# Attention logits from high and low halves: three products instead of four, the last as two 64-row matmuls

## The chip, the core and the metric

The kernel runs as one program on one core of one Trainium2 chip. The metric is the device time of one execution in microseconds (us). Five engines work side by side, each through its own queue in order: TensorE (PE in the profile, with its weight loads listed apart as PEld), VectorE (DVE), ScalarE (ACT), GpSimd (POOL) and SyncE (SP), which here only starts transfers (DMA).

## The reference, cut to what matters

One encoder layer is applied to two sequences, a prompt of 1024 rows and a sample of 2048 rows, both of width 1024. After a projection to eight parts, two attentions run over different parts:

```python
# window_gqa: 8 heads of 64, 2 key heads, blocks of 128 queries against 3 blocks of 128 keys
logits = einsum('bnqhgd,bnkhd->bnhgqk', qb, kw) * (HEAD_DIM ** -0.5)
logits = where(valid, logits + bias, NEG_INF);  p = softmax with a sink
# diff_attention: 4 heads, each with two maps (m) of 64, every query against all S keys
logits = einsum('bqhmd,bkhmd->bhmqk', qb, kh) * (HEAD_DIM ** -0.5)
p = softmax(logits + bias);  w = p[:, :, 0] - lam * p[:, :, 1]
out = rms_norm(einsum('bhqk,bkhe->bqhe', w, vh)) * (1 - lambda_init)
```

Then come a gate, the output projection and a layer norm. The contraction of every logit runs over only 64 elements.

## The kernel before, in words

All large matmuls run in a rounded 32-bit form (F32R). To keep accuracy, each operand is split in a high part and a low part, x = xH + xL, each rounded by itself, and a product is summed from several matmuls of the parts.

**Stages.** First the modulation and the input projections (`projections`, `step3`, lines 187 to 189: three matmuls of 128 rows by 512 columns for each step). Queries and keys go to DRAM in both parts: a tile's first 64 rows are high, the next 64 are low. In the last third of the projections the windowed attention (`windowed`, `first`, `second`) is interleaved with them: `beside()` sends projection steps to PE between its pieces. Then comes the differential attention (`slot`, `logits`, `transpose`, `values`), the sample's 4 heads first (64 units of 128 queries), then the prompt's (16 units, each of two blocks of queries against 1024 keys). Its first three units (EARLY) run among the last projections. The output projection (`outputs`) ends the kernel.

**Windowed logits.** For each head `first` takes one PSUM tile `lgA` of two and adds two matmuls of 128 rows: the weights are the head's queries [qH; qL], the moving side is the keys' high part in both halves of the partitions, then the low part in both halves (line 608). A VectorE pass (line 610) adds the bias and takes the minimum, and ScalarE takes the exponential.

**Differential logits.** A slot j of four in a unit works on one map m and half the keys: a PSUM tile `lg` of 128 by 1024 (two banks, c = 0 and 1), and for each bank two matmuls of 128 rows by 512 columns (line 822): the queries [qH; qL] (v = 0) and the same with the halves swapped, [qL; qH] (v = 1), both against [kH; kL]. That gives high by high, low by low, and both mixed products. VectorE adds the bias (line 827), ScalarE takes the exponential (835), GpSimd combines the two maps (844, 846). Three units later PE transposes the result (860), ScalarE and VectorE split it (862, 863), and PE multiplies it with the values (878 to 880).

**What sets the order.** PE's order around the change is written out by hand (`manual_schedule(engines={PE})`): in a slot the logits, then up to six value matmuls, then four transposes. The other engines' orders come from the framework's planner, which simulates the program. All transfers are started on SP's queue. Queries of the differential attention arrive in two layouts already (lines 780 to 782: the second one swapped by two transfers of 64 partitions each). Keys come by `load_keys` (line 751), the windowed queries by `load_block` (line 588).

Of the kernel before, what the change touches and what calls it, by code (L numbers as in the profile page):

```python
# [11 lines left out]
F32 = mybir.dt.float32  # L12
# [8 lines left out]
P = 128  # L21
D = 1024
KC = D // P
HD = 64
# [13 lines left out]
CH = 512  # L38
# [29 lines left out]
def hybrid_layer(ctx, tc, x_prompt, x_sample, c_prompt, c_sample, w_in, w_out, w_ada, b_ada, ln_g, ln_b,  # L68
                 attn_sink, lambda_q1, lambda_k1, lambda_q2, lambda_k2, subln_w, rel_bias, oh, eye,
                 y_prompt, y_sample):  # L70
    nc = tc.nc
# [3 lines left out]
    def pool(stack, name, bufs=1, space=None, side=None):  # L75
        if space is None:
            return stack.enter_context(tc.tile_pool(name=name, bufs=bufs, side=side, reuse_waits="tile"))
        if space == DRAM:
            return stack.enter_context(tc.tile_pool(name=name, bufs=bufs, space=space))
        return stack.enter_context(tc.tile_pool(name=name, bufs=bufs, space=space, side=side, reuse_waits="tile"))  # L80
# [15 lines left out]
    QA, KA, VA, GA, QB, KB, VB, GB, OT, OA = ([] for _ in range(10))  # L96
# [291 lines left out]
    def fill(n):  # L388
        for _ in range(n):
            next(steps, None)  # L390
# [110 lines left out]
    with tc.issue_after(wload[6]):  # L501
# [15 lines left out]
        for i in range(2):  # L517
            bg = sm2.tile([1, D], F32, tag="bg", name="bg")
            nc.sync.dma_start(out=bg, in_=b_ada[2 * D:3 * D].rearrange("(o d) -> o d", o=1))
            for q in range(2):  # L520
                cs = slice(q * 512, (q + 1) * 512)
# [12 lines left out]
    def windowed(upto):  # L534
# [3 lines left out]
        Bs, live, wait, n0 = {}, [], [], done.get(2, 0)  # L538
        total = (upto - n0) * 32
        Bs[0] = load_block(*order[0])  # L540
        count = [0, 0]

# [29 lines left out]
    def load_keys_of(s, i):  # L572
        T = SEQS[s] // P
        lo, hi = max(i - 1, 0), min(i + 1, T - 1)
        nb = hi - lo + 1
        nk = nb * P
        K = kv_p.tile([P, 2, 2, 384], F32R, tag="k", name="KAt")
        src = KA[s][:, :, :, lo * P:lo * P + nk].rearrange("n l d t -> d n l t")
        nc.sync.dma_start(out=K[0:HD, :, :, :nk].bitcast(F32), in_=src)
        nc.sync.dma_start(out=K[HD:P, :, :, :nk].bitcast(F32), in_=src)  # L580
        V = kv_p.tile([P, 3, 2 * P], F32R, tag="v", name="VAt")
        return dict(s=s, i=i, nb=nb, nk=nk, lo=lo, boff=(lo - (i - 1)) * P, K=K, V=V, l={})

    def load_block(s, i):
        B = load_keys_of(s, i)
        cs = slice(i * P, (i + 1) * P)
        B["Q"] = qa_p.tile([P, HA, P], F32R, tag="q", name="QAt")
        nc.sync.dma_start(out=B["Q"].bitcast(F32), in_=QA[s][:, :, cs].rearrange("h r t -> r h t"))
        k0, nb = B["lo"] * P, B["nb"]
        nc.sync.dma_start(out=B["V"][:, :nb].bitcast(F32),  # L590
                          in_=VA[s][k0:k0 + nb * P, :].rearrange("(b p) e -> p b e", p=P))
        B["G"] = qa_p.tile([P, 4, P], F32, tag="g", name="GAt")
        nc.sync.dma_start(out=B["G"], in_=GA[s][:, :, cs].rearrange("i r t -> r i t"))
        return B

    def first(B, n):

        nk, boff = B["nk"], B["boff"]
        nm = sA_p.tile([P, 4], F32, tag="nm", name="nmA")
        sm_ = sA_p.tile([P, 4], F32, tag="sm", name="smA")  # L600
        l = l_p.tile([P, 4, 386], F32, tag="l", name="l")
        nc.scalar.copy(l[:, :, 0:1], nsink[:, n * 4:n * 4 + 4].unsqueeze(2))
        B["l"][n] = l
        for h4 in range(4):
            h = n * 4 + h4
            L = ps_lgA.tile([P, 512], F32, tag="lgA", name="lgA")
            for hl in range(2):
                nc.tensor.matmul(L[:, :nk], lhsT=B["Q"][:, h, :], rhs=B["K"][:, n, hl, :nk],  # L608
                                 start=(hl == 0), stop=(hl == 1))
            nc.vector.tensor_tensor_reduce(  # L610
                out=l[:, h4, 1:1 + nk], in0=L[:, :nk], in1=tA[:, h, boff:boff + nk], scale=1.0,
                scalar=nsink[:, h:h + 1], op0=ALU.add, op1=ALU.min, accum_out=nm[:, h4:h4 + 1])
            nc.scalar.activation(l[:, h4, :1 + nk], l[:, h4, :1 + nk], AF.Exp, bias=nm[:, h4:h4 + 1], scale=-1.0,
                                 accum_out=sm_[:, h4:h4 + 1])
            if h4 == 3:
                rc = sA_p.tile([P, 4], F32, tag="rc", name="rcA")
                nc.vector.reciprocal(out=rc, in_=sm_)  # L617
                for q in range(4):
                    lv, r1 = l[:, q, 1:1 + nk], rc[:, q:q + 1]
                    if q == 1:  # L620
                        nc.scalar.activation(lv, lv, AF.Copy, scale=r1)
                    else:
                        nc.gpsimd.tensor_scalar(out=lv, in0=lv, scalar1=r1, scalar2=1.0, op0=ALU.mult, op1=ALU.mult)  # L623
            yield

    def second(B, n):
# [5 lines left out]
        def values(b):  # L632
            H, L = parts[b]
            v = B["V"][:, b, n * P:(n + 1) * P]
            nc.tensor.matmul(O, lhsT=v, rhs=H, start=(b == 0), stop=False)
            nc.tensor.matmul(O, lhsT=v, rhs=L, start=False, stop=(b == nb - 1))  # L636

        for b in range(nb + 2):
            if b > 1:
                values(b - 2)  # L640
            if b < nb:
# [3 lines left out]
                H = pa_p.tile([P, 512], F32R, tag="pth", name="pthA")  # L645
                L = pa_p.tile([P, 512], F32R, tag="ptl", name="ptlA")
                nc.scalar.copy(H, pt)
                nc.vector.tensor_tensor(out=L, in0=pt, in1=H.bitcast(F32), op=ALU.subtract)
                parts.append((H, L))
# [22 lines left out]
    ps_lgA = pool(ast, "ps_lgA", 2, PSUM)  # L672
# [54 lines left out]
    for s in (1, 0):  # L727
        T = SEQS[s] // P
        for h in range(HB):
            for i in range(0, T, 2):  # L730
                g = len(groups_of)
                n = len(units)
# [15 lines left out]
    def load_keys(s, h, some):  # L748
        for kq in some:
            kt = k_p.tile([P, 2, CH], F32R, name="kt")  # L750
            nc.sync.dma_start(out=kt.bitcast(F32),
                              in_=KB[s][h][:, :, kq * CH:(kq + 1) * CH].rearrange("m r t -> r m t"))
            heads[s, h][1].append(kt)

    def load_head(s, h):
# [41 lines left out]
    def logits(n, j):  # L797

        s, h, i, g = units[n]
        if n == j == 0:  # L800
            load_head(s, h)
            load_keys(s, h, range(2, SEQS[s] // CH))
            load_queries(g)
            fill(25)
        m, hf = 1 - j // 2, j % 2
        G = groups_[g]
        W, Kt, _ = heads[s, h]
        if "s0" not in G:
            G["s0"] = st_p.tile([P, 2], F32, tag="s0", name="s0g")
        if j == 0:  # L810
            rows[n] = {}
            stats[n] = (st_p.tile([P, 2, 2], F32, tag="nm", name="nm"), st_p.tile([P, 8], F32, tag="s1", name="s1"))
        if hf == 0:
            rows[n][m] = (r1_p if m else r0_p).tile([P, SMAX], F32, name=f"l{m}")
        nm, s1 = stats[n]
        row = rows[n][m]

        b, kt0 = (i % 2, hf * 2) if s else (hf, 0)
        L = ps_lg.tile([P, 1024], F32, name="lg")
        for c in range(2):  # L820
            for v in range(2):
                nc.tensor.matmul(L[:, c * CH:(c + 1) * CH], lhsT=G["Q"][:, v, m, b * P:(b + 1) * P],  # L822
                                 rhs=Kt[kt0 + c][:, m, :], start=(v == 0), stop=(v == 1))
        off = (1 - i) * P + hf * 1024 + LC if s else (1 - i - hf) * P + LC
        off = min(max(off, 0), LC + 384)
        half = row[:, hf * 1024:(hf + 1) * 1024]
        nc.vector.tensor_tensor_reduce(  # L827
            out=half, in0=L, in1=W[:, off:off + 1024], scale=1.0,
            scalar=nm[:, m, 0:1] if s and hf else 3e38, op0=ALU.add, op1=ALU.min, accum_out=nm[:, m, hf:hf + 1])
        if s and hf == 0:  # L830
            return
        c = 0 if s else hf
        sums = s1[:, c:c + 1] if m else G["s0"][:, b:b + 1]
        e = row if s else half
        nc.scalar.activation(e, e, AF.Exp, bias=nm[:, m, hf:hf + 1], scale=-1.0, accum_out=sums)  # L835
        if m == 1:
            nc.vector.reciprocal(out=s1[:, 2 + c:3 + c], in_=sums)
            return
        r = s1[:, 4 + c:5 + c]
        nc.vector.tensor_scalar(out=r, in0=sums, scalar1=s1[:, 2 + c:3 + c], scalar2=neglam, op0=ALU.mult,  # L840
                                op1=ALU.mult)
        for c in range(2) if s else (hf,):
            cs = slice(c * 1024, (c + 1) * 1024)
            nc.gpsimd.tensor_scalar(out=rows[n][1][:, cs], in0=rows[n][1][:, cs], scalar1=r, scalar2=1.0,  # L844
                                    op0=ALU.mult, op1=ALU.mult)
            nc.gpsimd.tensor_tensor(out=row[:, cs], in0=row[:, cs], in1=rows[n][1][:, cs], op=ALU.add)  # L846
# [322 lines left out]
```

## Time and profile before

| What | Value |
|---|---|
| median of 3 runs | 2135.27 us (2133.46 to 2138.25) |
| the profiled execution's own time | 2139.87 us |
| its span in the trace | 2138.1 us |
| PE busy | 2069.9 us, 97% |
| PEld busy | 1779.8 us, 83% |
| DVE busy | 1297.1 us, 61% |
| POOL busy | 1162.2 us, 54% |
| ACT busy | 1040.4 us, 49% |
| mean granted TensorE clock | 0.987 of full speed |

Busy time is the union of an engine's instructions. Matmuls are pipelined: the record of one lasts longer than the distance to the next, so PE's pace is read from the starts, and a busy PE is not one at its peak. The shares are means over the whole span; the stages differ, so the stretches are looked at one by one below.

### The profile page before, as it was taken

What the parts mean: (1) busy time and instruction counts of PE and PEld (TensorE: products, weight loads), DVE (VectorE), ACT (ScalarE), POOL (GpSimd) and SP (SyncE); (2) the same over time, 40 slices, a digit from 0 to 9 for tenths busy, and PEclk for the clock granted to TensorE, in tenths of its full rate; (3) what the DMA queues carried; (4) which work ended last, traced back from release to release, by engine and by line L of the source; (5) the groups of instructions that cost most, each with busy time, mean ns of one, the idle gap of its engine ahead of it and who ended that gap; (6) DMA issues with size and microseconds to landing.
All of it is one profiled execution on the core that took longest, in us unless ns stands there. A gap on an engine that the chain in (4) does not pass through costs nothing.

```text
span 2138.1 us, 32629 instructions
## 1 busy us (share of the span) xinstructions
PE 2069.9 (97%) x11597; PEld 1779.8 (83%) x11597; DVE 1297.1 (61%) x2534; ACT 1040.4 (49%) x2022; POOL 1162.2 (54%) x840
## 2 busy tenths in 40 slices
PE   7999999999999999999997999999999999699998
PEld 4777898888988888888886999999999998688887
DVE  5325224212225777677653999999999998455555
ACT  5211103011015777677632777777777897422221
POOL 3213213212124344343342889898898889777774
PEclk9999999999999999999998999999999999799999
DMA  9675635435538868778435123132231486767763
GB/s 270 180 258 182 181 128 167 130 124 135 154 117 226 203 173 213 196 209 216 144 113 161 38 81 78 47 101 57 84 77 38 116 163 84 140 163 204 196 195 103
DMA packets 340203, 312.46 MB, mean 146 GB/s; under 512 B 32086, under 2 KB 296950, under 8 KB 339656
## 3 DMA queue, kind: packets, MB, share of 16 engines
q1 hardware_dynamic: 340040, 310.37, 53.7%
q8 instruction: 92, 1.51, 0.4%
q14 instruction: 71, 0.58, 0.2%
HBM read 212.70 MB, written 97.60 MB: 145 GB/s over the span
## 4 chain that ended last, share of the span: by engine, by line
PE 85%; DMA 7%; POOL 2%; DVE 2%; issue 2%; ACT 1%; SPq 1%; DVEq 0%; POOLq 0%; ACTq 0%
PE lg L822 13%; PE pj L187 12%; PE pj L188 12%; PE pj L189 12%; PE tp L860 6%; PE po L1048 4%; PE po L1050 4%; PE po L1049 4%; PE ac L880 3%; PE ac L879 3%; PE ac L878 3%; PE lgA L608 3%; PE tp L644 3%; DMA Q<-qb 2%; PE ac L636 2%
## 5 line engine op out<-in xcount | busy, mean ns | idle before, releaser
L187 PE MATMUL pj<-uH,wH 128*128 128x512 f32 x1040 | 418.7, 403 | 6.0 <-DVE gg L258 6.0
L218 POOL TENSOR_TENSOR wL<-wr,wH 128x1024 fp32r<-128x1024 f32 x74 | 181.8, 2459 | 418.1 <-DVE wH L216 377.0
L189 PE MATMUL pj<-uH,wL 128*128 128x512 f32 x1040 | 407.7, 392 | 0.0
L188 PE MATMUL pj<-uL,wH 128*128 128x512 f32 x1040 | 407.1, 391 | 0.0
L822 PE MATMUL lg<-kt,Q 128*128 128x512 f32 x1280 | 379.3, 418 | 16.7 <-DMA Q<-qb 15.0
L846 POOL TENSOR_TENSOR l<-l,l 128x1024 f32<-128x1024 f32 x160 | 383.1, 2415 | 1.2
L835 ACT ACTIVATE l<-l,nm 128x2048 f32<-128x2048 f32 (+1 forms) x192 | 331.0, 1724 | 16.7 <-DVE nm L827 16.1
L822 PEld LDWEIGHTS lg<-kt,Q 128*128 128x128 f32 x1280 | 219.2, 191 | 48.3 <-issue 15.0
L844 POOL TENSOR_SCALAR l<-l,s 128x1024 f32<-128x1024 f32 x160 | 178.3, 1127 | 126.2 <-DVE s L840 68.3
L827 DVE CUSTOM_DVE_ANT_0 l<-lg,W 128x1024 f32<-128x1024 f32 x192 | 233.3, 1215 | 18.8 <-PE lg L822 18.4
L862 ACT CAST pth<-tp 128x512 fp32r<-128x512 f32 x320 | 186.2, 582 | 113.6 <-PE tp L860 108.5
L189 PEld LDWEIGHTS pj<-uH,wL 128*128 128x128 f32 x1040 | 195.5, 188 | 42.3
L187 PEld LDWEIGHTS pj<-uH,wH 128*128 128x128 f32 x1040 | 196.0, 188 | 39.2 <-DVE gg L258 6.8
L863 DVE TENSOR_TENSOR ptl<-tp,pth 128x512 fp32r<-128x512 f32 x320 | 209.2, 685 | 25.7 <-ACT pth L862 23.6
L188 PEld LDWEIGHTS pj<-uL,wH 128*128 128x128 f32 x1040 | 196.3, 189 | 31.0
L860 PE MATMUL tp<-ident,l 128*128 128x128 f32 x1280 | 195.0, 276 | 14.1 <-DVE ptl L863 14.1
L623 POOL TENSOR_SCALAR l<-l,rcA 128x384 f32<-128x384 f32 (+1 forms) x144 | 81.0, 581 | 190.7 <-DVE rcA L617 97.3
L880 PE MATMUL ac<-pth,vt 128*128 128x256 f32 x640 | 182.3, 285 | 0.0
L879 PE MATMUL ac<-ptl,vt 128*128 128x256 f32 x640 | 181.5, 284 | 0.0
L878 PE MATMUL ac<-pth,vt 128*128 128x256 f32 x640 | 181.2, 283 | 0.0
L827 DVE CUSTOM_DVE_ANT_0 l<-lg,W,nm 128x1024 f32<-128x1024 f32 x128 | 164.1, 1282 | 24.1 <-PE lg L822 17.0
L860 PEld LDWEIGHTS tp<-ident,l 128*128 128x128 f32 x1280 | 150.2, 142 | 17.0 <-DVE ptl L863 10.7
(210 smaller groups left out, 4031.6 us busy)
## 6 DMA issues: line engine op xcount, KB each, us to landing
wr<-in_w_in SPq DMA_DIRECT2D x39, 1024.0 KB
KAt<-ka SPq DMA_DIRECT2D x40, 384.0 KB
QAt<-qa SPq DMA_DIRECT2D x24, 512.0 KB
kt<-kb SPq DMA_DIRECT2D x24, 512.0 KB
Q<-qb SPq DMA_DIRECT2D x48, 256.0 KB
Q<-qb SPq DMA_DIRECT2D x96, 128.0 KB
vt<-vb SPq DMA_DIRECT2D x48, 256.0 KB
wa<-in_w_ada SPq DMA_DIRECT2D x32, 256.0 KB
```

Source lines behind the costliest of these rows:

```text
L187: nc.tensor.matmul(acc, lhsT=a(k), rhs=b(k), start=(k == 0), stop=False)
L188: nc.tensor.matmul(acc, lhsT=a(k), rhs=bl(k), start=False, stop=False)
L189: nc.tensor.matmul(acc, lhsT=al(k), rhs=b(k), start=False, stop=(k == KC - 1))
L822: nc.tensor.matmul(L[:, c * CH:(c + 1) * CH], lhsT=G["Q"][:, v, m, b * P:(b + 1) * P], rhs=Kt[kt0 + c][:, m, :], start=(v == 0), stop=(v = ...
L827: nc.vector.tensor_tensor_reduce(out=half, in0=L, in1=W[:, off:off + 1024], scale=1.0, scalar=nm[:, m, 0:1] if s and hf else 3e38, op0=ALU ...
L835: nc.scalar.activation(e, e, AF.Exp, bias=nm[:, m, hf:hf + 1], scale=-1.0, accum_out=sums)
L846: nc.gpsimd.tensor_tensor(out=row[:, cs], in0=row[:, cs], in1=rows[n][1][:, cs], op=ALU.add)
L860: nc.tensor.transpose(pt[:, c * P:(c + 1) * P], rows[n][0][:, (j * 4 + c) * P:(j * 4 + c + 1) * P], ident)
L863: nc.vector.tensor_tensor(out=L[:, :, qs], in0=p3, in1=H[:, :, qs].bitcast(F32), op=ALU.subtract)
L878: nc.tensor.matmul(a, lhsT=Vt[kq][:, 0, c, :], rhs=H[:, c, :], start=(kb == 0), stop=False)
L879: nc.tensor.matmul(a, lhsT=Vt[kq][:, 0, c, :], rhs=L[:, c, :], start=False, stop=False)
L880: nc.tensor.matmul(a, lhsT=Vt[kq][:, 1, c, :], rhs=H[:, c, :], start=False, stop=(kb == T - 1))
```

## The change: what it does

In both attentions the product of the two low parts is dropped. What is left for a logits tile is the two mixed products, or one mixed and the high one, in one matmul of 128 rows, and one product over 64 rows.

In the differential attention, bank c = 0 takes the swapped queries [qL; qH] against [kH; kL], which gives both mixed products; bank c = 1 takes the plain queries [qH; qL] against keys that are now stored swapped, [kL; kH]. After these two come two matmuls of 64 rows, high by high: bank 0 on partitions 0 to 63, bank 1 on partitions 64 to 127. For this `load_keys` loads every odd chunk of 512 keys with its halves swapped, by two transfers of 64 partitions in place of one.

In the windowed attention two heads are taken together, in both `lgA` tiles at once: two matmuls of 128 rows ([qH; qL] against the keys' high part in both halves), then two of 64 rows (qH against the keys' low part), the even head's on partitions 0 to 63 and the odd head's on 64 to 127. Odd heads' queries are loaded swapped, so `load_block` starts three transfers where it started one. VectorE's and all later work is the same.

```diff
@@ load_block
-        nc.sync.dma_start(out=B["Q"].bitcast(F32), in_=QA[s][:, :, cs].rearrange("h r t -> r h t"))
+        qe, qo = [QA[s].rearrange("(h e) r t -> e r h t", e=2)[e][:, :, cs] for e in range(2)]
+        q4 = B["Q"].rearrange("r (h e) t -> r h e t", e=2).bitcast(F32)
+        nc.sync.dma_start(out=q4[:, :, 0], in_=qe)
+        nc.sync.dma_start(out=q4[0:HD, :, 1], in_=qo[HD:P])
+        nc.sync.dma_start(out=q4[HD:P, :, 1], in_=qo[0:HD])
@@ first
-            L = ps_lgA.tile([P, 512], F32, tag="lgA", name="lgA")
-            for hl in range(2):
-                nc.tensor.matmul(L[:, :nk], lhsT=B["Q"][:, h, :], rhs=B["K"][:, n, hl, :nk],
-                                 start=(hl == 0), stop=(hl == 1))
+            if h4 % 2 == 0:
+                Ls = [ps_lgA.tile([P, 512], F32, tag="lgA", name="lgA") for _ in range(2)]
+                for e in range(2):
+                    nc.tensor.matmul(Ls[e][:, :nk], lhsT=B["Q"][:, h + e, :], rhs=B["K"][:, n, 0, :nk],
+                                     start=True, stop=False)
+                for e in range(2):
+                    rs = slice(e * HD, (e + 1) * HD)
+                    nc.tensor.matmul(Ls[e][:, :nk], lhsT=B["Q"][rs, h + e, :], rhs=B["K"][rs, n, 1, :nk],
+                                     start=False, stop=True)
+            L = Ls[h4 % 2]
@@ load_keys
-            nc.sync.dma_start(out=kt.bitcast(F32),
-                              in_=KB[s][h][:, :, kq * CH:(kq + 1) * CH].rearrange("m r t -> r m t"))
+            src = KB[s][h][:, :, kq * CH:(kq + 1) * CH].rearrange("m r t -> r m t")
+            if kq % 2:
+                nc.sync.dma_start(out=kt[0:HD].bitcast(F32), in_=src[HD:P])
+                nc.sync.dma_start(out=kt[HD:P].bitcast(F32), in_=src[0:HD])
+            else:
+                nc.sync.dma_start(out=kt.bitcast(F32), in_=src)
@@ logits
+        qs = slice(b * P, (b + 1) * P)
         for c in range(2):
-            for v in range(2):
-                nc.tensor.matmul(L[:, c * CH:(c + 1) * CH], lhsT=G["Q"][:, v, m, b * P:(b + 1) * P],
-                                 rhs=Kt[kt0 + c][:, m, :], start=(v == 0), stop=(v == 1))
+            nc.tensor.matmul(L[:, c * CH:(c + 1) * CH], lhsT=G["Q"][:, 1 - c, m, qs], rhs=Kt[kt0 + c][:, m, :],
+                             start=True, stop=False)
+        for c in range(2):
+            rs = slice(c * HD, (c + 1) * HD)
+            nc.tensor.matmul(L[:, c * CH:(c + 1) * CH], lhsT=G["Q"][rs, c, m, qs], rhs=Kt[kt0 + c][rs, m, :],
+                             start=False, stop=True)
```

## Rows read from the trace of the kernel before

**Rows 1.** The page's chain that ended last: shares of the span by engine and line.

```profile
PE 85%; DMA 7%; POOL 2%; DVE 2%; issue 2%; ACT 1%; SPq 1%; DVEq 0%; POOLq 0%; ACTq 0%
```

**Rows 2.** Busy time by stretch: windowed attention, then three stretches of the differential one.

```profile
core 0: us, PE busy (x) PEld busy (x) DVE busy (x) ACT busy (x) POOL busy (x), PEclk, DMA share, GB/s
670.00:1050.00 380.00, 376.39 (x2035) 319.39 (x2033) 268.58 (x709) 270.25 (x688) 151.26 (x181) 1.00 0.77 198
...
1250.00:1650.00 400.00, 400.00 (x2701) 366.00 (x2700) 370.42 (x711) 313.82 (x523) 352.16 (x220) 1.00 0.27 74
1650.00:1750.00 100.00, 100.00 (x681) 91.66 (x679) 94.03 (x199) 88.19 (x181) 90.12 (x59) 1.00 0.56 128
1750.00:1820.00 70.00, 65.03 (x434) 59.25 (x433) 58.06 (x132) 57.06 (x127) 60.62 (x41) 0.98 0.63 97
```

**Rows 3.** Groups by line with shapes kept apart: busy us, mean ns.

```profile
L822 PE MATMUL lg<-kt,Q 128*128 128x512 f32 x1280 | 379.3, 418 | 16.7 <-DMA Q<-qb 15.0 <-DVE gg L258 1.4 <-DVE nm L827 0.3
...
L608 PE MATMUL lgA<-KAt,QAt 128*128 128x384 f32 x320 | 84.6, 345 | 0.0
...
L608 PE MATMUL lgA<-KAt,QAt 128*128 128x256 f32 x64 | 13.1, 286 | 0.0
```

**Rows 4.** PE over one slot of the differential attention: start us, length us.

```profile
1502.04 0.60 PE L860 MATMUL tp<-ident,l 128*128 128x128 f32 x4
1502.40 1.16 PE L822 MATMUL lg<-kt,Q 128*128 128x512 f32 x4
1503.40 0.28 PE L878 MATMUL ac<-pth,vt 128*128 128x256 f32 x1
1503.51 0.28 PE L879 MATMUL ac<-ptl,vt 128*128 128x256 f32 x1
...
1504.11 0.60 PE L860 MATMUL tp<-ident,l 128*128 128x128 f32 x4
1504.47 1.18 PE L822 MATMUL lg<-kt,Q 128*128 128x512 f32 x4
```

**Rows 5.** PE where windowed logits stand between projections.

```profile
902.54 0.51 PE L608 MATMUL lgA<-KAt,QAt 128*128 128x384 f32 x2
902.88 0.39 PE L187 MATMUL pj<-uH,wH 128*128 128x512 f32 x1
```

**Rows 6.** PE, line 473's own lengths (ns min/median/max), and weight loads around it.

```profile
97.47 0.39 PE L188 MATMUL pj<-uL,wH 128*128 128x512 f32 x1
97.70 0.39 PE L189 MATMUL pj<-uH,wL 128*128 128x512 f32 x1
98.02 1.02 PE L473 MATMUL ac<-ohs,rbx 33*8 33x512 f32 x2
98.97 0.50 PE L187 MATMUL pj<-uH,wH 128*128 128x512 f32 x1
99.31 0.39 PE L188 MATMUL pj<-uL,wH 128*128 128x512 f32 x1
...
L473 PE MATMUL ac<-ohs,rbx x4: 588/590/592, 98.0 to 107.8; 33*8 33x512 f32 x2, 33*4 33x512 f32 x2
...
97.48 0.19 PEld L189 LDWEIGHTS pj<-uH,wL 128*128 128x128 f32 x1
98.02 0.09 PEld L473 LDWEIGHTS ac<-ohs,rbx 33*8 33x8 f32 x2 [0.35 <-issue]
98.97 0.19 PEld L187 LDWEIGHTS pj<-uH,wH 128*128 128x128 f32 x1 [0.86 <-DVE eL L285]
99.08 0.19 PEld L188 LDWEIGHTS pj<-uL,wH 128*128 128x128 f32 x1
```

**Rows 7.** PE around the 4-row matmuls of line 452.

```profile
48.91 0.40 PE L189 MATMUL ac<-uH,wL 128*128 128x512 f32 x1
49.24 1.05 PE L452 MATMUL pmt<-sel,mrow 4*128 4x2 f32 x8
50.22 0.50 PE L187 MATMUL ac<-uH,wH 128*128 128x512 f32 x1
50.55 0.40 PE L188 MATMUL ac<-uL,wH 128*128 128x512 f32 x1
```

**Rows 8.** PE around the 128-row, 2-column matmuls of lines 525 and 526.

```profile
185.92 0.39 PE L189 MATMUL pj<-uH,wL 128*128 128x512 f32 x1
186.15 0.40 PE L525 MATMUL ac<-gH,onesr 128*2 128x512 f32 x1
186.38 0.40 PE L526 MATMUL ac<-gL,onesr 128*2 128x512 f32 x1
186.62 0.39 PE L187 MATMUL pj<-uH,wH 128*128 128x512 f32 x1
```

**Rows 9.** Waits of PE from 1650 to 1830: us in total, times, longest.

```profile
PE tp L860 <- DVE ptl L863: 3.8, 4, 1.4
PE lg L822 <- DMA Q<-qb: 3.5, 1, 3.5
```

**Rows 10.** DMA issues on SP's queue by line: lines 588, 780 and 781, ns min/median/max.

```profile
L588 SPq DMA_DIRECT2D QAt<-qa x24: 359/366/1351, 219.7 to 1022.0; - x24
L780 SPq DMA_DIRECT2D Q<-qb x48: 359/360/2000, 1061.8 to 1789.2; - x48
L781 SPq DMA_DIRECT2D Q<-qb x48: 579/579/1707, 1063.4 to 1790.1; - x48
```

## The prediction

> **What bounds the kernel now.** I read first the chain that ended last: 85% of the span is PE's, every other engine at most 2%, DMA 7% [rows 1]. Then the busy time by stretch, because the change touches two stages only. In the windowed stage PE is busy 376.4 of 380 us and no other engine passes 75%; in the sample's part of the differential attention PE is busy 400 of 400 us, but VectorE stands at 370.4 (93%) and GpSimd at 352.2 (88%) close behind [rows 2]. So PE's time is the kernel's time in both places, and in the second there is little room before VectorE is the bound. [...] Last I read PE's own starts, since its records overlap: four logits matmuls take from 1502.40 to the next value matmul at 1503.40, and a slot's period is 2.07 us [rows 4]. A matmul of 128 rows by 512 columns in a run of equals takes 0.23 us from start to start (97.47 to 97.70), and its weights are loaded during the one before it (97.48) [rows 6].
>
> **What goes.** 1280 logits matmuls in the differential attention make 320 tiles of four [rows 3]. If the two 64-row matmuls of a tile share one pass, one pass of 0.23 us goes from each: 320 x 0.23 = 73.6 us. In the windowed attention 384 matmuls make 96 pairs of heads, 80 with 384 columns and 16 with 256. A pass of 384 columns takes (902.88 - 902.54) / 2 = 0.17 us [rows 5]; one of 256 takes 0.12 (1503.40 to 1503.51, [rows 4]). That is 80 x 0.17 + 16 x 0.12 = 15.5 us. So 89 us of PE's passes go at most.
>
> **What comes: the crossings.** The new order on PE goes from 128 rows to 64 and back once in each tile and pair. The trace before has no 64-row F32R matmul, but it has PE crossing from 128 rows to fewer and back, at line 473 (33 rows) and line 452 (4 rows). In: the matmul after 97.70 does not start 0.23 later but at 98.02, 0.32 later, and its weight load starts only then, not at 97.70 [rows 6]; at 48.91 to 49.24 it is 0.33 [rows 7]. So 0.09 us are lost and the load is no longer hidden. Out: line 473's second record starts at 98.02 + 1.02 - 0.59 (the median length of one record) = 98.45 and, with 0.43 between the two, its pass ends at 98.88; the next load and matmul start at 98.97, 0.09 later. That matmul's record is 0.50 instead of 0.39 and the next one starts 0.34 after it instead of 0.23: the uncovered load costs 0.11 [rows 6]. The same 0.50 and 0.33 follow line 452 [rows 7]. A round trip of F32R matmuls of 128 columns of weights therefore costs 0.09 + 0.11 + 0.09 + 0.11 = 0.40 us. Changing only the columns, 128 to 2 and back, costs nothing: the starts stay 0.23 apart [rows 8].
>
> Two doubts. Lines 452 and 473 are also the kernel's only products in full 32 bits, so the wait could belong to that form and not to the rows; the transposes, full 32 bits too, meet F32R matmuls without such a gap (0.36 for four, [rows 4]), so I take it for the rows. If it is not, a crossing costs 0. And the second half's weights have to be loaded too, 0.11 if after the first half's, 0 if beside it; no row shows two loads into different rows, so I take the middle, 0.05.
>
> [...]
>
> **The sum.** A differential tile: 0.40 + 0.05 - 0.23 = +0.22 us; 320 x 0.22 = 70.4. PE was idle some 5 us in the prompt's part (7.3 us of waits, [rows 9]), and this takes up added time: 65. A windowed pair: 0.40 + 0.05 - 0.17 = +0.28 (80 of them) or 0.40 + 0.05 - 0.12 = +0.33 (16): 27.7. Together +93 us on the profiled execution's 2139.9, so 2233; the median lies 4.6 us under that execution, which gives 2228.
>
> **Edits at nothing.** The transfers: `load_block` starts three instead of one, 24 times, at 0.36 to 0.58 us of SP's queue each [rows 10], some 0.8 to 1.2 us more in a block that lasts about 16 us (380 / 24), a block ahead of its use; 12 odd key chunks are two transfers instead of one. Bytes and row lengths stay. Prefetch hides them; uncovered they would cost at most 24 x 1.2 = 29 us, and less than nothing isn't to be had. What queues behind them on SP are the block's values and gates, needed later still. The wait for two free `lgA` tiles instead of one: PE has projections between its logits in this stage [rows 5], and VectorE is at 71% [rows 2], so both tiles are long free; if not, PE's queue waits for one more pass of line 610, with projections held behind it. VectorE, ScalarE and GpSimd do the same work in the same shapes. That the planner lays their orders out anew I put at 0, give or take 5 us.
>
> **The rivals.** *No crossing cost, VectorE becomes the bound (faster).* The 64-row loads are pulled ahead and the halves run together. PE's unit of four slots falls from 8.28 to 8.28 - 4 x 0.23 = 7.36 us. VectorE needs 0.926 x 8.28 = 7.67 for a unit [rows 2], so it decides from there. It works in order and waits for ScalarE inside the unit, so I put it at 97% busy: 7.91. The sample's 61 units after the early three gain 61 x 0.37 = 23 us, the prompt's part (VectorE at 94%) 5, the early three units 12 x 0.23 = 3, the windowed pairs 15.5: 47 us, 2088. With VectorE at 100% it is 2071, with no gain in the differential attention 2116. For it: that the wait at lines 452 and 473 may be the 32-bit form's. Against it: every crossing of rows that I looked at has the wait, in both directions.
>
> [...]
>
> *The halves run one after the other (slower still).* Then no pass is saved, the second load hides behind the first half, and each round trip costs its 0.40: 320 x 0.40 - 5 + 96 x 0.40 = 161, so 2296. This is also the case in which the change doesn't do what it says. For it: no row shows two matmuls in the array at once. [...]
>
> *The wait without the uncovered loads.* Only 2 x 0.09 are paid: 0.18 - 0.23 = -0.05 for a tile, about 0 for a pair: 320 x -0.05 = -16, so 2119; with half of the loads uncovered 0.18 + 0.11 + 0.05 - 0.23 = +0.11, 35 us, and about 15 more from the pairs: 2185.
>
> **How the numbers follow.** The forecast, crossings as in rows 6 and 7 with the halves side by side, 0.45: 2228, its own range 2205 (second load hidden: 0.17 a tile, 0.23 or 0.28 a pair, +72) to 2253 (second load in full: 0.28, 0.34 and 0.39, +118). VectorE as the bound 0.37: 2071 to 2116. The wait without loads or with half of them 0.10: 2115 to 2190. One after the other 0.08: around 2296. Range 2075 to 2258: it leaves out the last case, a little of the fastest and the odd case above, under 0.2. Measurement can tell about 0.2% (4 us) from no change. Faster: 0.37 and half of 0.10, 0.42; slower: 0.45, 0.08 and nearly half of 0.10, 0.55; the same 0.03.
>
> **What would show it.** In the changed trace: in a slot, the first 64-row matmul about 0.32 us after the second mixed one, with its load at the same moment; the two 64-row starts about 0.1 apart; the next value matmul about 0.9 to 0.95 us after the second mixed one (0.69 before); a record of 0.39 in place of 0.28 for that value matmul; a slot's period of about 2.29 us with PE busy throughout and VectorE down to some 84%. The forecast is wrong if the loads of the 64-row matmuls start with the matmul before them, if the period falls under 2.07 with VectorE near 97%, or if the 64-row starts lie 0.23 or more apart.

## The result and the profile after

The changed kernel takes 2207.18 us (median of 4 executions; one of them, 4091.93 us, was disturbed and is left out of the ratio) against 2136.76 us before: 1.0314 times as long, 95% interval 1.0295 to 1.0333. That is +70 us; +93 was forecast, in a range that holds the measured time. The profiled execution took 2199.95 us, 2198.2 of it in the span.

One slot of the changed kernel on PE, and a narrower window that shows the second mixed matmul's own start (start us, length us):

```profile
1501.08 0.60 PE L880 MATMUL tp<-ident,l 128*128 128x128 f32 x4
1501.44 0.71 PE L838 MATMUL lg<-kt,Q 128*128 128x512 f32 x2
1502.08 0.50 PE L842 MATMUL lg<-kt,Q 64*128 64x512 f32 x2
1502.52 0.39 PE L898 MATMUL ac<-pth,vt 128*128 128x256 f32 x1
1502.74 0.28 PE L899 MATMUL ac<-ptl,vt 128*128 128x256 f32 x1
...
1503.34 0.60 PE L880 MATMUL tp<-ident,l 128*128 128x128 f32 x4
1503.69 0.72 PE L838 MATMUL lg<-kt,Q 128*128 128x512 f32 x2
...
1501.76 0.40 PE L838 MATMUL lg<-kt,Q 128*128 128x512 f32 x1
```

The weight loads of the same slot, and the 64-row matmuls' own lengths over the whole kernel (ns min/median/max):

```profile
1501.41 0.30 PEld L838 LDWEIGHTS lg<-kt,Q 128*128 128x128 f32 x2
1502.08 0.19 PEld L842 LDWEIGHTS lg<-kt,Q 64*128 64x128 f32 x2 [0.37 <-issue]
1502.51 0.19 PEld L898 LDWEIGHTS ac<-pth,vt 128*128 128x128 f32 x1 [0.25 <-issue]
...
L842 PE MATMUL lg<-kt,Q x640: 490/496/793, 1096.6 to 1878.2; 64*128 64x512 f32 x160
```

To be seen here, beside [rows 4]: the period is 2.25 us (1501.44 to 1503.69) where it was 2.07, though a pass is gone. The second mixed matmul starts at 1501.76 and the 64-row pair at 1502.08, 0.32 later instead of 0.23, with its loads only then. The pair's two records together last 0.50, and one alone 0.496: they start together (3 to 4 ns apart by the trace's own starts, in all 416 pairs), and so do their loads (two in 0.19, one is 0.18). The value matmul behind them starts at 1502.52 with a record of 0.39 instead of 0.28, and its load again starts with it, not before.

The same stretches as in [rows 2], the later ones moved to where the stage now lies:

```profile
670.00:1050.00 380.00, 378.10 (x1922) 288.12 (x1920) 257.04 (x673) 255.19 (x655) 144.61 (x174) 1.00 0.75 194
...
1300.00:1700.00 400.00, 398.03 (x2494) 291.07 (x2493) 351.92 (x657) 289.75 (x483) 322.58 (x202) 1.00 0.25 65
1700.00:1800.00 100.00, 100.00 (x630) 73.20 (x628) 88.26 (x182) 81.27 (x157) 86.77 (x56) 1.00 0.52 114
```

PE is as full as before and gets less done: 2494 instead of 2701 matmuls in 400 us. VectorE (third pair) falls from 370 to 352 us and GpSimd from 352 to 323, so neither set the pace. The granted clock is 1.00 in all three stretches.

### The profile page after: what moved, and what is told of

Read it like the earlier page. It is cut to its first block, busy times and chain, and to the rows that moved or that the text cites. A ratio compares the mean times of both kernels' runs of the same rounds, so it can differ in the third digit from the quotient of the medians.

```text
span 2198.2 us, 32677 instructions
## 1 busy us (share of the span) xinstructions
PE 2134.6 (97%) x11597; PEld 1672.3 (76%) x11597; DVE 1311.1 (60%) x2534; ACT 1037.5 (47%) x2022; POOL 1160.2 (53%) x840
## 4 chain that ended last, share of the span: by engine, by line
PE 87%; DMA 6%; DVE 2%; POOL 2%; issue 1%; SPq 1%; ACT 1%; DVEq 0%; POOLq 0%; ACTq 0%
PE pj L187 12%; PE pj L188 11%; PE pj L189 11%; PE lg L838 7%; PE lg L842 6%; PE tp L880 6%; PE ac L898 6%; PE po L1068 4%; PE po L1070 4%; PE po L1069 4%; PE ac L900 3%; PE ac L899 3%; PE tp L655 3%; PE ac L646 2%; PE lgA L618 2%; PE ac L647 1%
## 5 line engine op out<-in xcount | busy, mean ns | idle before, releaser
L187 PE MATMUL pj<-uH,wH 128*128 128x512 f32 x1040 | 427.5, 411 | 4.2 <-DVE gg L258 4.2
L838 PE MATMUL lg<-kt,Q 128*128 128x512 f32 x640 | 228.6, 437 | 16.9 <-DMA Q<-qb 12.5
L883 DVE TENSOR_TENSOR ptl<-tp,pth 128x512 fp32r<-128x512 f32 x320 | 220.2, 689 | 37.5 <-ACT pth L882 29.0
L898 PE MATMUL ac<-pth,vt 128*128 128x256 f32 x640 | 213.0, 333 | 0.0
L900 PE MATMUL ac<-pth,vt 128*128 128x256 f32 x640 | 180.8, 283 | 0.0
L898 PEld LDWEIGHTS ac<-pth,vt 128*128 128x128 f32 x640 | 120.5, 188 | 73.8 <-issue 55.6
```

The source lines that it names most:

```text
L187: nc.tensor.matmul(acc, lhsT=a(k), rhs=b(k), start=(k == 0), stop=False)
L838: nc.tensor.matmul(L[:, c * CH:(c + 1) * CH], lhsT=G["Q"][:, 1 - c, m, qs], rhs=Kt[kt0 + c][:, m, :], start=True, stop=False)
L883: nc.vector.tensor_tensor(out=L[:, :, qs], in0=p3, in1=H[:, :, qs].bitcast(F32), op=ALU.subtract)
L898: nc.tensor.matmul(a, lhsT=Vt[kq][:, 0, c, :], rhs=H[:, c, :], start=(kb == 0), stop=False)
L900: nc.tensor.matmul(a, lhsT=Vt[kq][:, 1, c, :], rhs=H[:, c, :], start=False, stop=(kb == T - 1))
```

## The experiments

The theory after the result: a tile that goes from 128 rows to 64 and back pays 0.40 us (twice 0.09 of wait, twice 0.11 of a load that nothing covers), the two halves share one pass of 0.23, so a tile saves 0.23 and pays 0.40. The stage lengths below run from the first start of the stage's logits matmuls to the last one, from the views of single lines; before they are 735.2 us for the differential attention:

```profile
L822 PE MATMUL lg<-kt,Q x1280: 387/397/776, 1080.5 to 1815.7; 128*128 128x512 f32 x183
```

and 376.1 us for the windowed one:

```profile
L608 PE MATMUL lgA<-KAt,QAt x384: 277/337/424, 672.8 to 1048.9; 128*128 128x384 f32 x160, 128*128 128x256 f32 x32
```

**One part alone: the differential attention.** `load_block` and `first` are as before.

```diff
-        qe, qo = [QA[s].rearrange("(h e) r t -> e r h t", e=2)[e][:, :, cs] for e in range(2)]
...
+        nc.sync.dma_start(out=B["Q"].bitcast(F32), in_=QA[s][:, :, cs].rearrange("h r t -> r h t"))
```

> Only the differential attention is changed, the windowed one is as before. Theory (each tile pays 0.40 us for going from 128 rows to 64 and back, the two halves share one pass of 0.23 us): +0.17 us for each of 320 tiles, less 5 us of idle time that it takes up, so +50 us, about 2187; the slot lasts 2.25 us as in the changed kernel. Rival (most of the loss comes from the windowed pairs, which need two PSUM tiles at once): under +15 us.

Measured: 2185.11 us against 2134.89, +50, ratio 1.024 (1.0216 to 1.0264). The stage lasts 784.8 us, +49.6, and the slot 2.25 us (median of the starts):

```profile
L827 PE MATMUL lg<-kt,Q x640: 387/398/776, 1076.1 to 1860.9; 128*128 128x512 f32 x160
```

So this part pays +0.155 for each of 320 tiles, as the theory has it, and it makes most of the loss.

**The other part alone: the windowed attention.** The mirror of that edit: `load_keys` and `logits` as before.

> Only the windowed attention is changed, the differential one is as before. Theory: a pair of heads saves one pass of 0.17 us and pays 0.40, +0.23 us for each of 96 pairs, so +20 to +22 us, about 2158, and no wait of TensorE for a PSUM tile. Rival (waiting for two free PSUM tiles): +50 us or more, with waits of TensorE on the VectorE pass of the logits in the list of waits.

Measured: 2148.28 us, +13, ratio 1.0071 (1.005 to 1.0092, 11 to 20 us), less than expected. The stage runs from 667.3 to 1060.3 (393.0, +16.9), and a pair in it looks like this:

```profile
906.12 0.52 PE L614 MATMUL lgA<-KAt,QAt 128*128 128x384 f32 x2
906.57 0.45 PE L618 MATMUL lgA<-KAt,QAt 64*128 64x384 f32 x2
906.95 0.50 PE L187 MATMUL pj<-uH,wH 128*128 128x512 f32 x1
907.28 0.39 PE L188 MATMUL pj<-uL,wH 128*128 128x512 f32 x1
...
L618 PE MATMUL lgA<-KAt,QAt x192: 379/436/443, 668.3 to 1060.3; 64*128 64x384 f32 x160, 64*128 64x256 f32 x32
```

From 906.12 to 906.95, and 0.11 more for the projection's uncovered load, are 0.94 us, where four passes of [rows 5] take 0.68: +0.26 with these rounded figures. By the medians of all starts a pair of 384 columns pays 0.09 on the way in, 0.19 on the way out and 0.105 at the matmul behind, and saves 0.174: +0.22; one of 256 columns pays +0.27. That is 21.6 us for 96 pairs, as the expectation has it. The stage itself grew by 16.9: some 1.6 us of other matmuls now lie outside its first and last logits, PE's idle time in it falls from 3.6 to 2.7 us, and about 2 us are not placed. In PE's waits from 660 to 1070 none is for a logits tile (the longest sum is 1.2 us, for a split on VectorE), so the rival with two PSUM tiles falls.

**Are the halves really run at once?** Both 64-row matmuls on partitions 0 to 63, keys unswapped.

```diff
-            rs = slice(c * HD, (c + 1) * HD)
-            nc.tensor.matmul(L[:, c * CH:(c + 1) * CH], lhsT=G["Q"][rs, c, m, qs], rhs=Kt[kt0 + c][rs, m, :],
+            rs = slice(0, HD)
+            nc.tensor.matmul(L[:, c * CH:(c + 1) * CH], lhsT=G["Q"][rs, 0, m, qs], rhs=Kt[kt0 + c][rs, m, :],
```

> As the differential-only kernel, but both 64-row matmuls of a tile use partitions 0 to 63 (the odd key chunks are loaded unswapped, by one transfer). Theory (different halves really run at once): here the second one must follow the first, 0.23 us more for a tile, 320 x 0.40 - 5 = +123 us, about 2260, and their starts lie 0.23 us apart. Rival (the halves gain nothing from lying apart): the same time as the differential-only kernel, about 2187.

Measured: 2257.00 us, +122, ratio 1.0583 (1.0561 to 1.0604); the stage lasts 855.5 us (1076.1 to 1931.6), +120. The pair's two records now last 0.73 where the first alone lasts 0.50. By the trace's starts the second begins 0.34 after the first, a pass of 0.23 and the first's uncovered load of 0.11; its own load is covered, so the way out is 0.11 shorter, and the tile pays 0.23 more in all:

```profile
1502.50 0.73 PE L827 MATMUL lg<-kt,Q 64*128 64x512 f32 x2
1503.16 0.38 PE L883 MATMUL ac<-pth,vt 128*128 128x256 f32 x1
...
1502.50 0.50 PE L827 MATMUL lg<-kt,Q 64*128 64x512 f32 x1
...
1502.50 0.29 PEld L827 LDWEIGHTS lg<-kt,Q 64*128 64x128 f32 x2 [0.36 <-issue]
```

In different halves the second matmul is worth 72 us of the kernel's time, 0.225 for a tile: there it costs nothing.

**The saved pass without the crossing.** Three matmuls of 128 rows in a tile; bank 1 keeps its mixed products alone and lacks the high by high and the low by low one.

```diff
-        for c in range(2):
-            for v in range(2):
+        for c, v in ((0, 1), (1, 1), (0, 0)):
...
-                                 rhs=Kt[kt0 + c][:, m, :], start=(v == 0), stop=(v == 1))
+                             rhs=Kt[kt0 + c][:, m, :], start=(v == 1), stop=(v == 0 or c == 1))
```

> The kernel before with three matmuls of 128 rows in a differential tile instead of four: bank 1's high by high and low by low products are left out. It is the saved pass without any change of the row count. Theory: TensorE needs 1.84 us for a slot, VectorE's 7.67 us for a unit decides, 7.9 for a unit of four slots, about -31 us, 2106. Rival (nothing else bounds): 320 x 0.23 = -74 us, 2063. Rival (VectorE's waits already set the pace): no gain, 2134 to 2137.

Measured: 2088.55 us, -46, ratio 0.9792 (0.9769 to 0.9815); the stage is 681.8 us, -53:

```profile
1300.00:1600.00 300.00, 298.41 (x2059) 271.64 (x2058) 295.65 (x583) 262.18 (x426) 287.94 (x181) 1.00 0.30 74
...
PE tp L859 <- DVE ptl L862: 25.5, 9, 8.6
```

The time lies between the first two expectations, and neither came. VectorE is now close to its limit, at 295.7 of 300 us (98.5%, not 97), and GpSimd is at 96%. PE's usual slot falls by the whole pass, 2.08 to 1.86 us (medians from 1300 to 1700 us), but the mean only from 2.11 to 1.95: some transposes start late, and PE's waits for VectorE there are 25.5 us over the whole kernel instead of 14.1. So the saved pass was there to be had and worth 46 us of the kernel's time; the crossings turned that into +50.

**The crossing without a saved pass.** The kernel before, its fourth matmul cut to 64 rows (bank 1 lacks one of its mixed products).

```diff
+        for c, v in ((0, 0), (1, 0), (0, 1), (1, 1)):
+            rs = slice(0, 64 if c and v else P)
+            nc.tensor.matmul(L[:, c * CH:(c + 1) * CH], lhsT=G["Q"][rs, v, m, b * P:(b + 1) * P],
+                             rhs=Kt[kt0 + c][rs, m, :], start=(v == 0), stop=(v == 1))
```

> The kernel before with its four matmuls in a differential tile, but the last of them (bank 1, swapped queries) runs over 64 rows only, partitions 0 to 63: the other mixed product of bank 1 is left out. Still four passes, no two matmuls at once, windowed attention as before. Theory (the change of the row tile is what costs): a round trip of 0.40 us for each tile, 320 x 0.40 - 5 = +123 us, about 2260. Rival (two 64-row matmuls at once disturb each other, or their loads do): no change, 2137.

Measured: 2252.37 us against 2132.32, +120, ratio 1.0551 (1.0535 to 1.0566): 0.375 for a tile, with nothing run at once. The usual slot grows by 0.40 (medians 2.08 and 2.48 us); the total is a little less because PE's idle time takes some of it up. The edit also turns the order of the matmuls; the next run has the same order without the loss.

```profile
1502.74 0.18 PEld L822 LDWEIGHTS lg<-kt,Q 64*128 64x128 f32 x1 [0.38 <-issue]
1503.17 0.19 PEld L878 LDWEIGHTS ac<-pth,vt 128*128 128x128 f32 x1 [0.25 <-issue]
```

From the 64-row load to the next load are 0.43 us for one matmul; for two in different halves they were 0.43 too (1502.08 to 1502.51 above). The second half adds nothing to the crossing.

**96 rows instead of 64.** The same edit with 96 in place of 64 (half of that mixed product is left out).

> As the kernel with the last matmul of a tile over 64 rows, but over 96 rows (partitions 0 to 95), which no 64-row half of the array can hold; a part of the second mixed product of bank 1 is left out. Theory (the wait belongs to the array being split in halves): no change, 2137, weights loaded during the matmul before. Rival (any matmul over fewer rows than the one before pays): +123 us, about 2260.

Measured: 2132.30 us against 2132.32, ratio 0.9996 (0.9984 to 1.0007).

```profile
1499.82 0.39 PE L822 MATMUL lg<-kt,Q 96*128 96x512 f32 x1
1500.05 0.28 PE L878 MATMUL ac<-pth,vt 128*128 128x256 f32 x1
...
1499.82 0.19 PEld L878 LDWEIGHTS ac<-pth,vt 128*128 128x128 f32 x1
```

The value matmul's load starts at 1499.82, with the 96-row matmul, and is covered; that matmul itself has a record of 0.39, so its own load was covered too. So it isn't fewer rows as such that cost: 64 rows, which fit a half of the array, do (0.375 us a tile), and 96, which don't, do not (ratio 0.9996). With 64 rows the wait is 0.09 us each way; with 96 none shows (0.23 from that matmul to the value matmul).

**The 64-row pair first.** In each tile the two loops change places, and the flags with them.

```diff
+        for c in range(2):
+            rs = slice(c * HD, (c + 1) * HD)
+            nc.tensor.matmul(L[:, c * CH:(c + 1) * CH], lhsT=G["Q"][rs, c, m, qs], rhs=Kt[kt0 + c][rs, m, :],
+                             start=True, stop=False)
...
+                             start=False, stop=True)
```

> Differential attention only, with the two 64-row matmuls before the two of 128 rows instead of behind them. Theory: the load behind the transposes was uncovered by about 0.08 us already in the kernel before (0.31 instead of 0.23 us to the second logits matmul), so the way in costs 0.08 to 0.09 less: +0.09 us for a tile, 320 x 0.09 - 3 = +26 us, about 2163. Rival (order does not matter, a round trip costs its 0.40): as the differential-only kernel, about 2187.

Measured: 2186.44 us, +54, ratio 1.0244 (1.0229 to 1.0259): my theory's saving of 0.09 did not come, the rival's 2187 did.

```profile
1501.88 0.60 PE L869 MATMUL tp<-ident,l 128*128 128x128 f32 x4
1502.41 0.50 PE L828 MATMUL lg<-kt,Q 64*128 64x512 f32 x2
1502.84 0.72 PE L831 MATMUL lg<-kt,Q 128*128 128x512 f32 x2
1503.40 0.28 PE L887 MATMUL ac<-pth,vt 128*128 128x256 f32 x1
```

From the transposes to the pair are 0.53 us instead of the 0.36 to a 128-row matmul ([rows 4]); behind the mixed ones the value matmul is covered again (0.28). In the kernel before, the first load behind the transposes ran during the last of them (both from 1502.37) and the first logits matmul started 0.03 behind that one's start, so the 0.08 that I had counted as uncovered was only the length of a record that starts early, and no time to be won.

**Half as many crossings.** Two tiles' matmuls together, the four narrow ones first, then the four wide ones (from the fourth unit on).

```diff
+            if hf == 0:
+                Lp[:] = [ps_lg.tile([P, 1024], F32, name="lg") for _ in range(2)]
+                for narrow in (True, False):
+                    for x in range(2):
+                        tile_mms(Lp[x], x, narrow)
+            L = Lp[hf]
```

> Differential attention only: the matmuls of two tiles together, first the four of 64 rows, then the four of 128, so one change of rows for two tiles (the first three units keep one tile at a time); both PSUM tiles of the logits have to be free at once. Theory: two tiles take 0.20 + 0.46 + 0.20 + 0.92 = 1.78 us of TensorE instead of 2.00, -0.11 us a tile, 308 x -0.11 = -34 us, about 2105, bounded by VectorE. Rival (the wait for both PSUM tiles takes it back: VectorE needs 2.5 us to free them, TensorE has 2.15 us of other work meanwhile): 0.3 to 0.5 us for two tiles, so 2120 to 2165.

Measured: 2151.22 us, +19, ratio 1.0072 (1.005 to 1.0095): 31 us less loss than with one tile at a time (+50, the differential part alone), but no gain over the kernel before. Two groups in a row, PE's waits for keys over the whole kernel, and a stretch of the stage:

```profile
1508.30 1.86 PE L831 MATMUL lg<-kt,Q 64*128 64x512 f32 x8
1512.40 1.86 PE L831 MATMUL lg<-kt,Q 64*128 64x512 f32 x8
...
PE lg L831 <- DMA kt<-kb: 10.1, 6, 2.8
...
1250.00:1350.00 100.00, 95.73 (x634) 79.27 (x632) 88.59 (x169) 76.72 (x122) 83.22 (x53) 0.97 0.32 81
```

Two slots last 4.10 us here, 0.04 less than in [rows 4] (0.06 by the medians) and not 0.22, though no wait stands in them. Two passes of 0.23 go and one crossing of 0.40 comes: 0.06. The rest of my 0.22 was 0.08 counted twice as uncovered time, the mistake of the run before this one. Nor is it the rival's wait for both PSUM tiles that makes the loss: for VectorE's pass over the second tile PE waits 1.9 us in the whole stage. That the time lies in the rival's 2120 to 2165 is chance. What the trace shows is waits for key chunks, which a group asks for one slot earlier: 10.1 us, where PE's list of the kernel before has none. They come at three changes of head, and right there, from 1271, 1411 and 1548 us, the granted clock is 0.50 for 3.4 to 6.8 us. From 1250 to 1750 us its mean is 0.98 (0.97 to 0.99 in stretches of 100 us), where [rows 2] have 1.00: 4% of the time at half the clock, an estimated 10 us.

**The same with the wide ones first.** The two flags and the order of the loop are turned.

```diff
-                for narrow in (True, False):
+                for narrow in (False, True):
```

> Two tiles with one change of rows as in the kernel before this one, but the four matmuls of 128 rows come first and the four of 64 rows last, and the value matmuls follow. By TensorE's pitches: two tiles cost 0.12 + 0.92 + 0.20 + 0.46 + 0.20 us and another 0.09 where transposes now meet value matmuls, 1.99 instead of 2.07 us, -0.08 us for 154 pairs of tiles, -12 us, 2120; with the 10 us of waits for key chunks, which are asked for earlier, about 2130. Rival (with both PSUM tiles in one group TensorE loses its lead over VectorE, whatever the order): as with the narrow ones first, about 2150.

Measured: 2154.14 us against 2130.07, +24, ratio 1.0109 (1.0092 to 1.0127). The order doesn't give it back.

```profile
1501.72 0.38 PE L899 MATMUL ac<-pth,vt 128*128 128x256 f32 x1
1504.04 1.84 PE L831 MATMUL lg<-kt,Q 128*128 128x512 f32 x8
1505.81 0.38 PE L899 MATMUL ac<-pth,vt 128*128 128x256 f32 x1
```

In a stretch without waits a group needs 1.77 us (1504.04 to 1505.81), and two slots 4.09 (1501.72 to 1505.81), so the group as such would gain 0.05 in either order. The waits for keys (12.5 us) and a granted clock of 0.98 from 1250 to 1750 us take more. The rival's number came, but its reason, PE's lost lead over VectorE, shows only in part: PE waits 1.8 us for the second tile and 6.4 us at the transposes, where it was 3.8. No version of these beats the kernel before, and none was left that I expected to.

**Was it the rows at line 473?** The kernel before with line 473's operands padded with zero rows to 128.

```diff
-        rbx = sm2.tile([N_BUCKETS + 1, HA + HB], F32, name="rbx")
+        rbx = sm2.tile([P, HA + HB], F32, name="rbx")
...
-            ohs = sm2.tile([N_BUCKETS + 1, NREL], F32, tag="ohs", name="ohs")
+            ohs = sm2.tile([P, NREL], F32, tag="ohs", name="ohs")
```

> The kernel before with the full 32-bit matmuls of line 473 padded with zero rows from 33 to 128 rows; nothing else changes. Theory (the row tile is what waits): the padded matmul starts 0.23 us after the one before it and its weights are loaded during that one; no 0.09 us gap behind it. Rival (the full 32-bit form is what waits): 0.32 us, and the 0.50 us record behind it, as before. The total stays at 2130 to 2140 either way.

Measured in a single execution: 2131.18 us against 2130.07. The matmul is line 475 here:

```profile
98.23 0.39 PE L189 MATMUL pj<-uH,wL 128*128 128x512 f32 x1
98.54 1.02 PE L475 MATMUL ac<-ohs,rbx 128*8 128x512 f32 x2
99.50 0.50 PE L187 MATMUL pj<-uH,wH 128*128 128x512 f32 x1
99.83 0.39 PE L188 MATMUL pj<-uL,wH 128*128 128x512 f32 x1
```

With all 128 rows the wait is still there: 0.31 in, the same 0.50 and 0.33 behind. So at line 473 the full 32-bit form (here with 8 columns of weights) suffices for the wait, and the rival of this run holds. What 33 rows in F32R would cost, no run shows, and line 452 was not tried.

## Why the prediction was right, by its steps

- *PE is the bound and stays it.* So it was: 398 of 400 us busy, VectorE down to 88% (84% was forecast), no new wait of PE for a PSUM tile in its list.
- *The crossing costs 0.40 us.* The size held: 0.32 in, uncovered loads at both ends, 0.375 for a tile (0.40 in the usual slot) by the kernel with the crossing alone. That it held was luck in part: it was read from other rows. Lines 473 and 452 differ from their neighbours in rows and in the 32-bit form, and of this first doubt I took the wrong side for line 473: the form waits by itself. That 64-row F32R matmuls wait as well, at nearly the same price, is shown by 64 against 96 rows in one form, and was not shown by anything before. The argument from the transposes did not hold either: they are 32 bits and don't wait (0.12 us from the last value matmul to the first of them, 0.03 from the start of the last one to that of the first logits matmul, 1502.37 to 1502.40), but the full 32-bit matmul of 128 rows does (0.31 instead of 0.23). One sign of the forecast was off by its own terms: the value matmul was to start 0.9 to 0.95 after the second mixed one, but 0.11 of the crossing falls behind that start; the terms give 0.80, and 0.76 was measured.
- *The second half's load, 0.05 us.* This is the mis-sized term. It measured 0: both loads start together, and one 64-row matmul or two take the same 0.43. It stands in 320 tiles and 96 pairs: 0.05 x 416 = 21 us, nearly all of the 23 by which the forecast lay too high. The lower end of its own range was worked out with this load hidden; its +72 give 2207 to 2208, not the 2205 written there, and 2207.18 was measured.
- *The halves share a pass.* Right: apart they cost nothing, in one half 72 us more. The starts that I had put 0.1 us apart lie within 0.004. The loads into the two halves take 0.19 us together, where one takes 0.18; at the change from 128 rows the load starts only with its matmul (1502.08).
- *The parts.* Differential +50 where 65 was forecast, windowed +13 (11 to 20) where 27.7 was; with the load at 0 the same terms give 49 and 23, and the windowed pairs' starts add up to 21.6.
- *Edits at nothing.* The third query transfer shows in no wait of PE in the windowed stage; the SP queue issues the three in 0.37, 0.62 and 0.61 us. The swapped keys were not quite nothing: PE waits 3.0 us for key chunks in the changed kernel and 4.9 with the differential part alone, and not at all in the kernel before or with unswapped keys (both matmuls in one half). The 5 us of idle time that the forecast took off are offset by that.
- *The rival with VectorE as the bound* was right about what lies behind the crossing, VectorE near its limit (98.5% busy): without a crossing 2088.55 us for the differential part alone. I had put that part at 31 us, and it was 46; that the rival's 2088, windowed part included, is the same number is chance.

## What to carry to other kernels

Matmuls over 64 rows in the two halves of the array ran at once here (starts 3 to 4 ns apart) and cost one pass of 0.23 us, weight loads included (two in 0.19 us, one in 0.18). But going from F32R matmuls of 128 rows to such a pair and back cost 0.40 us, on the engine that is the bound, more than a pass of 512 columns (0.23): count the crossings against the passes saved. Two passes behind one crossing save 0.46 for 0.40, so here they could gain almost nothing, and what the larger group asks for earlier (here its keys, 10.1 us of waits) can cost more than that. And a price read from rows that differ from the new operation in two things is a guess at which of the two it belongs to, even when it comes out right.

## What the runs showed that I had not expected

- A full 32-bit matmul of 128 rows and 8 columns of weights among F32R ones waits as a 64-row one does: 0.31 us instead of 0.23 to its start, and 0.50 instead of 0.39 for the record behind it.
- A matmul of 96 rows among 128-row ones costs nothing (ratio 0.9996, 0.9984 to 1.0007).
- Weight loads into the two halves start together: two take 0.19 us where one takes 0.18, and two into the same half 0.29.
- Waits of PE for keys (10.1 us in six waits, the longest 2.8), at three changes of head, went with a granted clock of 0.50 for 3.4 to 6.8 us each (two tiles in one group, narrow ones first).
